# SwiGLU gating on one core: the first tile's store cut into 4 KiB and 28 KiB per partition

## The chip, the cores and the metric

One core of a Trainium2 chip. The time is device microseconds of one execution, the median over several. The profiled span is about 1.8 us shorter than the time of the same execution (933.9 against 935.7), so the two are not mixed below.

## The reference

```python
x: (8192, 8192) float32
a, b = np.split(x, 2, axis=-1)
return a * (b / (1 + np.exp(-b)))          # (8192, 4096) float32
```

268 MB are read and 134 MB written, with three operations per output element.

## The kernel before

Two rows of `x` are laid side by side in one partition, so a tile is 128 partitions of 64 KiB, and its result 32 KiB per partition, written over the front of the tile. Three tiles fit. SyncE issues the loads, ScalarE the stores of all but the last two tiles. Each of these two engines has its own queue of transfers, called a ring below: SyncE's (q1 in the profile) is the load ring, ScalarE's (q10) the store ring.

```python
R, BUFS = 2, 3
xv = x.tensor.reshape([N // R, R * M]).ap()
ov = out.tensor.reshape([N // R, R * half]).ap()

def swiglu(i, k, c0=0, cw=half):            # row k of tile i
    b = xt[:, k * M + half + c0 : ...]
    nc.scalar.activation(out=b, in_=b, func=_SILU)
    nc.vector.tensor_mul(out=xt[:, k * half + c0 : ...], in0=xt[:, k * M + c0 : ...], in1=b)

def store(i, c0=0, cw=R * half):
    (nc.scalar if i < last - 1 else nc.sync).dma_start(
        out=ov[i * P : (i + 1) * P, c0 : c0 + cw], in_=tiles[i][:, c0 : c0 + cw])

nc.vector.memset(zt, 0.0)                              # zt: 128 x 128
nc.scalar.dma_start(out=ov[0:P, 0:128], in_=zt)        # the early zero store, overwritten later

for i in range(BUFS):
    load(i)
for i in range(last):
    for k in range(R):
        swiglu(i, k)
    if i == last - 1:
        swiglu(last, 0)
    store(i)
    nxt = i + BUFS
    if nxt < last:
        load(nxt)
    ...                                                # the last tile is loaded by rows
... # cut: the last tile, in halves of a row, and its two stores
```

Of the kernel before, what the change touches and what calls it, by code (L numbers as in the profile page):

```python
# [1 line left out]

# [4 lines left out]

_SILU = mybir.ActivationFunctionType.Silu


@with_exitstack
def kernel(
    ctx: ExitStack,
    tc: tile.TileContext,
    x: bass.AP,
    out: bass.AP,
):




    nc = tc.nc
    N, M = x.shape
    half = M // 2
    P = nc.NUM_PARTITIONS
    R = 2
    BUFS = 3

    xv = x.tensor.reshape([N // R, R * M]).ap()  # L30
    ov = out.tensor.reshape([N // R, R * half]).ap()
    ntiles = N // (P * R)
    last = ntiles - 1

    pool = ctx.enter_context(tc.tile_pool(name="sbuf", bufs=BUFS))
    tiles = {}

    def load(i, rows=None):
        if i not in tiles:
            tiles[i] = pool.tile([P, R * M], x.dtype, name="xt")  # L40
        lo, hi = (0, R) if rows is None else rows
        nc.sync.dma_start(  # L42
            out=tiles[i][:, lo * M : hi * M], in_=xv[i * P : (i + 1) * P, lo * M : hi * M]
        )

    def swiglu(i, k, c0=0, cw=half):
        xt = tiles[i]
        b = xt[:, k * M + half + c0 : k * M + half + c0 + cw]
        nc.scalar.activation(out=b, in_=b, func=_SILU)  # L49
        nc.vector.tensor_mul(  # L50
            out=xt[:, k * half + c0 : k * half + c0 + cw],
            in0=xt[:, k * M + c0 : k * M + c0 + cw],
            in1=b,
        )

    def store(i, c0=0, cw=R * half):
        (nc.scalar if i < last - 1 else nc.sync).dma_start(
            out=ov[i * P : (i + 1) * P, c0 : c0 + cw], in_=tiles[i][:, c0 : c0 + cw]
        )


    zt = ctx.enter_context(tc.tile_pool(name="zeros", bufs=1)).tile([P, 128], x.dtype, name="zt")
    ctx.enter_context(tc.manual_schedule())
    nc.vector.memset(zt, 0.0)  # L64
    nc.scalar.dma_start(out=ov[0:P, 0:128], in_=zt)

    for i in range(BUFS):
        load(i)
    for i in range(last):
        for k in range(R):  # L70
            swiglu(i, k)
        if i == last - 1:
            swiglu(last, 0)
        store(i)
        nxt = i + BUFS
        if nxt < last:
            load(nxt)
        elif nxt == last:
            load(last, (0, 1))
            load(last, (1, 2))  # L80

    store(last, 0, half)
    for c0 in range(0, half, half // 2):
        swiglu(last, 1, c0, half // 2)
    store(last, half, half)


# [1 line left out]
_INS = ['x']  # L89
_OUTS = [((8192, 4096), 'float32')]  # L90


# [23 lines left out]
```

## Time and profile before

| | before |
|---|---|
| time, median of 3 | 935.86 us (935.71 to 936.21) |
| VectorE, ScalarE busy | 30%, 25% |
| packets of the two DMA queues | 68.6% + 31.2% of 16 engines' span |
| mean rate | 431 GB/s |

The DMA row and the two queue lines come first here, because they say that there is almost no idle time to win. The compute engines wait for data, and their idle time costs nothing. The prediction shows the lines and reads them. A "packet" below is one entry of the trace's DMA records, with its queue, start and duration. In this kernel it is one row of one partition, or the 4 bytes that report a transfer's end on one engine.

### The profile page before, as it was taken

The numbers are of one execution on the slowest core, as the hardware profiler recorded it, in microseconds if no ns is written. First come the engines' busy times: TensorE is split into PE (matmuls) and PEld (weight loads), VectorE is DVE, ScalarE is ACT, GpSimd is POOL, SyncE is SP. The second block draws the span as 40 slices with busy tenths as digits, with TensorE's granted clock in tenths as the row PEclk, the third lists the DMA queues.
The fourth block names the chain that finished last, engine by engine and source line by source line (L and its number), as shares of the span: only waits on it lengthen the run. The fifth ranks groups of instructions, "written<-read, shape, count | busy, mean of one in ns | idle before, by whom it ended". The sixth has DMA issues, their size and how long they took to land.

```text
span 933.9 us, 370 instructions
## 1 busy us (share of the span) xinstructions
DVE 283.5 (30%) x66; ACT 229.4 (25%) x66; POOL 0.2 (0%) x4
## 2 busy tenths in 40 slices
DVE  0333312333113332133321333213332133331252
ACT  0323330233312333113331133311333203332041
POOL 0000000000000000000000000000000000000000
DMA  9999999999999999999999999999999999999998
GB/s 407 422 413 460 411 431 441 449 427 420 456 408 445 431 431 441 435 422 441 448 414 436 435 451 425 429 443 414 446 427 436 436 432 425 439 451 411 441 434 383
DMA packets 9650, 402.74 MB, mean 431 GB/s; under 512 B 1072, under 2 KB 1200, under 8 KB 1200
## 3 DMA queue, kind: packets, MB, share of 16 engines
q1 hardware_dynamic: 5184, 276.83, 68.6%
q10 hardware_dynamic: 4464, 125.90, 31.2%
q14 instruction: 2, 0.02, 0.0%
HBM read 268.44 MB, written 134.28 MB: 431 GB/s over the span
## 4 chain that ended last, share of the span: by engine, by line
DMA 84%; DVE 10%; ACT 4%; DVEq 0%; issue 0%; SPq 0%; ACTq 0%
DMA out_dram<-xt 43%; DMA xt<-in_x_dram 41%; DVE xt L50 10%; ACT xt L49 4%; DVEq L111 0%; SPq L42 0%; ACTq L49 0%; DVEq L50 0%
## 5 line engine op out<-in xcount | busy, mean ns | idle before, releaser
L50 DVE TENSOR_TENSOR xt<-xt 128x4096 f32<-128x4096 f32 (+1 forms) x65 | 283.3, 4360 | 635.8 <-ACT xt L49 632.6
L49 ACT ACTIVATE xt<-xt 128x4096 f32<-128x4096 f32 (+1 forms) x65 | 228.1, 3556 | 686.5 <-DMA xt<-in_x_dram 686.5
L49 ACT ACT_TABLE_LOAD x1 | 1.3, 1283 | 1.5 <-DVE zt L64 1.5
L64 DVE MEMSET zt<- 128x128 f32 x1 | 0.2, 165 | 0.8 <-PEq L100 0.8
L100 POOL MEMSET const-bfloat16-1.0<- 128x1 bf16 x1 | 0.1, 101 | 0.0
L100 POOL MEMSET const-uint8-127<- 128x1 uint8 x1 | 0.1, 101 | 0.0
L100 POOL MEMSET const-float32-0.0<- 128x1 f32 x1 | 0.1, 98 | 0.2 <-issue 0.2
L100 POOL MEMSET const-float32-1.0<- 128x1 f32 x1 | 0.1, 98 | 0.0
## 6 DMA issues: line engine op xcount, KB each, us to landing
out_dram<-xt ACTq DMA_DIRECT2D x30, 4096.0 KB, 40.0
xt<-in_x_dram SPq DMA_DIRECT2D x2, 4096.0 KB, 26.8
out_dram<-xt SPq DMA_DIRECT2D x1, 4096.0 KB, 23.6
out_dram<-xt SPq DMA_DIRECT2D x2, 2048.0 KB, 14.5
xt<-in_x_dram SPq DMA_DIRECT2D x31, 34.2
out_dram<-zt ACTq DMA_DIRECT2D x1, 64.0 KB, 24.1
```

What stands on the lines that cost most here:

```text
L49: nc.scalar.activation(out=b, in_=b, func=_SILU)
L50: nc.vector.tensor_mul(out=xt[:, k * half + c0 : k * half + c0 + cw], in0=xt[:, k * M + c0 : k * M + c0 + cw], in1=b,)
L64: nc.vector.memset(zt, 0.0)
L100: nc = _bacc.Bacc("TRN2", target_bir_lowering=False, num_devices=1)
```

## The change

The intent: some output leaves as soon as the first row of the first tile is multiplied, rather than after both rows, so that the store ring starts earlier and with small packets.

```diff
-    def swiglu(i, k, c0=0, cw=half):
+    def swiglu(i, k, c0=0, cw=half, gated=None):
         nc.scalar.activation(out=b, in_=b, func=_SILU)
+        if gated:
+            gated()
         nc.vector.tensor_mul(...)
 ...
     for i in range(last):
-        for k in range(R):
-            swiglu(i, k)
+        swiglu(i, 0)
+        if i == 0:
+            swiglu(i, 1, gated=lambda: store(0, 0, half // 4))
+        else:
+            swiglu(i, 1)
         if i == last - 1:
             swiglu(last, 0)
-        store(i)
+        if i == 0:
+            store(i, half // 4, R * half - half // 4)
+        else:
+            store(i)
```

## The prediction

> **What bounds the kernel now.** I read the page's busy line first, then its DMA queues, then the stretches of time, then the chain and the first 75 us of the timeline.
>
> The page of before:
>
> ```profile
> DVE 283.5 (30%) x66; ACT 229.4 (25%) x66; POOL 0.2 (0%) x4
> ...
> DMA  9999999999999999999999999999999999999998
> ...
> q1 hardware_dynamic: 5184, 276.83, 68.6%
> q10 hardware_dynamic: 4464, 125.90, 31.2%
> ...
> HBM read 268.44 MB, written 134.28 MB: 431 GB/s over the span
> ...
> out_dram<-xt ACTq DMA_DIRECT2D x30, 4096.0 KB, 40.0
> ...
> xt<-in_x_dram SPq DMA_DIRECT2D x31, 34.2
> ```
>
> VectorE and ScalarE are idle for 70% or more. The 16 DMA engines are at 90% or more in 39 of 40 slices, and the packets of the two queues fill 68.6 + 31.2 = 99.8% of their span. q1 carries what SyncE issues (all loads, the last three stores), q10 what ScalarE issues (the other stores). A store takes 40.0 us from issue to landing and a load 34.2, though either alone would need 4.19 MB / 431 GB/s = 9.7 us or 19.5 us: most of it is queueing behind the other ring and behind the transfer ahead.
>
> Now the stretches, with busy times of the engines, then the DMA share and GB/s at the end of a line:
>
> ```profile
> 100.00:400.00 300.00, 91.01 (x21) 77.37 (x22) 0.00 (x0) 1.00 1.00 432
> 400.00:700.00 300.00, 94.85 (x22) 72.19 (x21) 0.00 (x0) 1.00 1.00 435
> ...
> 35.40:45.70 10.30, 0.00 (x0) 0.01 (x1) 0.00 (x0) 1.00 0.95 366
> ...
> 932.00:934.00 2.00, 0.00 (x0) 0.00 (x0) 0.00 (x0) 1.00 0.02 8
> ```
>
> From 100 us on the share is 1.00. What isn't full is the start, the stretch in which the first store joins (366 GB/s; a stretch this short also has some rounding of packets at its edges) and the 2.0 us after the last bytes. The timeline gives the start that the change touches:
>
> ```profile
> 22.77 7.12 ACT L49 ACTIVATE xt<-xt 128x4096 f32<-128x4096 f32 x2 [20.03 <-DMA xt<-in_x_dram]
> 26.42 8.95 DVE L50 TENSOR_TENSOR xt<-xt 128x4096 f32<-128x4096 f32 x2 [25.43 <-ACT xt L49]
> 35.40 0.34 ACTq L57 DMA_DIRECT2D out_dram<-xt  x1
> 45.69 7.12 ACT L49 ACTIVATE xt<-xt 128x4096 f32<-128x4096 f32 x2 [15.79 <-DMA xt<-in_x_dram]
> ```
>
> The packet records of the same trace are more exact. A load row of 64 KiB is one packet and takes 2.418 us on its engine, a store row of 32 KiB 1.213 us, a 512 B row of the zero store 0.027 us, and from about 40 us on each engine takes one packet of q1, one of q10, and so on. Each engine has 256 x 2.418 + 256 x 1.213 = 929.5 us of packets, and the last of them ends 929 to 930 us after the first began. So the span is the sum of the packets, plus some 1.2 us before the first, plus some 2 us of landing after the last, plus two small excesses: the first load packet is 0.4 to 0.9 us too long, and the load packet that is under way when the first 32 KiB store packets arrive (36 to 39 us) takes 3.0 to 3.6 us instead of 2.418, some 0.6 to 1.1 us once, with up to 1 us more one packet later on a few engines; about 1.0 us on each. I call that the entry bubble. It is all of the 933.9 us that the change can reach.
>
> The chain of waits says "DMA 84%; DVE 10%": store, load of the same buffer, SiLU, two multiplies, store. That loop takes 40.4 + 33.8 + 3.6 + 2 x 4.4 = 86.7 us for three tiles, 28.9 us a tile, and the packets of one tile take 8 x (2.418 + 1.213) = 29.05 us. It is one loop seen twice: the landings are long because the engines are full. Shortening the compute part of it would only lengthen the queueing.
>
> **What the Trainium skill says.** "DMA: Bandwidth & Descriptors", section "Issuing engines are not separate DMA queues", says that transfers run on the same 16 DMA engines and interleave, whichever engine issued them. The trace agrees: 431 GB/s with two queues, and either queue alone also runs at 2.418 us per 64 KiB. The same page, "Queues, rings and completion order", says that an engine takes the queues in turn at packet granularity; the trace agrees one packet for one packet, and this makes the packet size the store's share. The page's "Where 436 GB/s comes from" puts the ceiling at 435.2 GB/s; the stretch from 400 to 700 us shows 435. No page that I read has the entry bubble.
>
> **The change, part by part.**
>
> (a) Removed: nothing. Instructions: ScalarE's stream has one DMA issue more (0.34 us on ScalarE's sequencer, before a wait for VectorE that it has anyway). The second SiLU is issued ahead of the new store, so the store doesn't hold it up. The compiled order shows otherwise the same operations in the same order on every engine. The new first part takes over the wait for the zero store (landed at about 25 us, so it costs nothing); the second part waits for VectorE alone, not for the first part; the load into the first buffer waits for both parts.
>
> (b) Moved: the first 4 KiB of each row leave when the first multiply ends, 26.42 + 4.43 = 30.85 us, not at 35.40, so 4.5 us earlier, while two loads are queued and the engines are busy. No byte is added, and nothing idles there that the early bytes could fill.
>
> (c) Added packets: 8 per engine. From the two sizes, 2 x 1.213 - 2.418 = 0.008 us is the fixed part of one, and 4 KiB and 28 KiB take about 0.16 and 1.06 us. Eight extra plus one more completion: 8 x 0.008 + 0.01 = under 0.1 us.
>
> (d) Changed interleaving. Working through one engine by hand: eight 4 KiB packets, each behind a 2.418 us load packet, occupy the store ring from about 34 us to 52. The 28 KiB packets queue behind them in order and start about 54.5 us, where before the first store was half done. The second and third loads, less slowed, end about 41.7 (before 44.5) and 65.0 (before 73.5). The first store ends about 70.3, not 66.2, so the fourth load is issued about 72 us, not 69.8, and the load ring is empty from 65 to 73: four or five packets of the next store (issued about 55.5) run alone. The engine remains full throughout. After that both rings are fed again, loads with a lead of about 10 us (before 3.7), stores with about 3 (before 8). That is the same stock of three buffers, placed otherwise: store landings should fall from 40.0 to about 34 us and load landings rise from 34.2 to about 40.
>
> (e) End: the last two stores of SyncE stand behind the last load in the same ring, and 9.7 + 4.9 us of their packets cover the compute of the last half row, 6.5 us from landing to issue. That slack of several us isn't touched.
>
> Sum: +0.1 us of packets, +0 of idle engines, and the entry bubble, which I can't derive: 1.0 us is there now.
>
> **The rivals.**
>
> 1. The bubble shrinks. The 512 B packets of the zero store entered at about 7 us and left the load packets beside them at 2.418, so the bubble goes with the size of the entering packet. If 4 KiB enters nearly free and 28 KiB then finds a ring that is already running, 0.6 to 0.9 us are won: 935.1.
>
> 2. The bubble only moves to the first 28 KiB packet, being the filling of a second stream's buffering: +0.1 us, 935.95. For it: the bubble comes to about 1 us, near the time of one 32 KiB packet.
>
> 3. The bubble belongs to any ring that restarts beside a running one. Then the load ring's restart at about 73 us adds another, and a store ring that falls dry once or twice another: +0.5 to +1.8 us, 936.4 to 937.6. Against it: in the tail the other ring ends and the stream goes from loads to stores without a gap; but no restart after 40 us exists in before.
>
> 4. A large loss from the late first store (a load ring dry for 8 us). If nothing else filled the engines, +8 us, 944. Against it: the second store is in the queue since about 56 us, and it fills them. Even this would be within 2%.
>
> 5. A gain from earlier store bytes, 4.5 us off the chain and so 931. Against it: the engines have 929.5 us of packets, and the ends cost over 3.
>
> **Range and chances.** Weights 0.35 for rival 1, 0.35 for 2, 0.25 for 3 and little for the rest give a middle of 935.9. The three runs of before lie 0.5 us apart, which widens both sides a little: 935.0 to 937.1. Faster by 2% would mean 917 us, below the sum of the packets: 0.003. Slower by 2% would need 19 us of idle engines or slower packets: 0.007. Within 2%: 0.99.
>
> **What would show it.** The timeline of the changed kernel should have two ScalarE store issues at about 30.9 and 35.4 us, the second SiLU pair of tile 1 about 43 instead of 45.7, and the wait of the fourth load ending near 72. The DMA row should stay at nines, the steady stretch at 432 to 435 GB/s. Median landings should be swapped, about 34 for stores and 40 for loads. The packet records should show bubbles (or none) at 34 and 54 us (rivals 1 and 2) and at 73 us (rival 3). I'd be wrong if a stretch after 100 us has a share under 1.00, if the 64 KiB packets are longer than 2.418 us in the new phase, or if the last store is issued so late that the final stretch has a gap.

## The result

The changed kernel took 936.72 us (median of 6, 936.36 to 936.88), the kernel before 935.79 us in the same rounds (median of 6, 935.67 to 936.65). The ratio is 1.0008, with a 95% interval of 0.9995 to 1.0021: the same within 2%. A ratio here is the mean time of one kernel's fast runs over that of the other's fast runs of the same rounds, so it isn't quite the ratio of the medians.

The page of the changed kernel, the lines that answer to those of before:

```profile
DVE 283.4 (30%) x66; ACT 229.4 (25%) x66; POOL 0.2 (0%) x4
...
DMA  9999999999999999999999999999999999999998
...
q1 hardware_dynamic: 5184, 276.83, 68.5%
q10 hardware_dynamic: 4608, 125.90, 31.2%
...
HBM read 268.44 MB, written 134.28 MB: 431 GB/s over the span
...
out_dram<-xt ACTq DMA_DIRECT2D x29, 4096.0 KB, 34.4
...
out_dram<-xt ACTq DMA_DIRECT2D x1, 3584.0 KB, 37.6
out_dram<-xt ACTq DMA_DIRECT2D x1, 512.0 KB, 24.5
xt<-in_x_dram SPq DMA_DIRECT2D x31, 39.8
```

The bytes are the same, and q10 has 144 packets more: 128 rows and 16 completions. The engines are as full as before. The first part of 0.5 MB needed 24.5 us from issue to landing, and the median landings have changed places (stores 40.0 to 34.4, loads 34.2 to 39.8).

The timeline of the changed kernel (start and length in us, engine, line, operation):

```profile
26.52 8.95 DVE L52 TENSOR_TENSOR xt<-xt 128x4096 f32<-128x4096 f32 x2 [25.53 <-ACT xt L49]
30.98 4.87 ACTq L59 DMA_DIRECT2D out_dram<-xt  x2
42.71 7.12 ACT L49 ACTIVATE xt<-xt 128x4096 f32<-128x4096 f32 x2 [12.71 <-DMA xt<-in_x_dram]
...
68.92 7.12 ACT L49 ACTIVATE xt<-xt 128x4096 f32<-128x4096 f32 x2 [19.09 <-DMA xt<-in_x_dram]
...
73.22 51.02 SPq L42 DMA_DIRECT2D xt<-in_x_dram  x3
...
106.28 7.12 ACT L49 ACTIVATE xt<-xt 128x4096 f32<-128x4096 f32 x2 [30.24 <-DMA xt<-in_x_dram]
```

The two store issues begin at 30.98 us. The second tile is there at 42.71 instead of 45.69, and the third at 68.92 instead of 74.56, because the store ring's small packets take little from them. The price is the fourth load: its issue waits for the first store until 73.22 us, and its tile is there at 106.28 instead of 103.71. The lines of before:

```profile
69.83 29.28 SPq L42 DMA_DIRECT2D xt<-in_x_dram  x2
74.56 7.12 ACT L49 ACTIVATE xt<-xt 128x4096 f32<-128x4096 f32 x2 [21.75 <-DMA xt<-in_x_dram]
...
103.71 7.12 ACT L49 ACTIVATE xt<-xt 128x4096 f32<-128x4096 f32 x2 [22.03 <-DMA xt<-in_x_dram]
```

Steady state, from 100 us on:

```profile
100.00:400.00 300.00, 88.99 (x21) 75.36 (x22) 0.00 (x0) 1.00 1.00 435
400.00:700.00 300.00, 96.85 (x22) 74.20 (x21) 0.00 (x0) 1.00 1.00 435
```

The DMA share is 1.00, as before.

One engine, worked out from the packet records (start in us and duration in ns; L is a load, S a store, with KiB; us are counted here from 1.25 us before the first load packet, which is within half a microsecond of the profile's):

```
before   34.02 L64 2418 | 36.44 L64 3272 | 39.71 S32 1213 | 40.92 L64 2424 | 43.34 S32 1213 | ...
after    34.10 L64 2418 | 36.52 S4 159 | 36.67 L64 2418 | 39.09 S4 159 | 39.24 L64 2418 | ...
         52.25 L64 2418 | 54.67 L64 3211 | 57.88 S28 1062 | 58.94 L64 2418 | 61.35 S28 1062 | ...
         65.89 S28 | 66.95 S28 | 68.00 S28 | 69.06 S28 | 70.12 S28 | 71.19 S32 | 72.40 S32 |
         73.61 S32 | 74.82 S32 | 76.03 S32 | 77.23 L64 2418 | 79.65 S32 1213 | ...
```

The 4 KiB packets enter without stretching the load packets beside them. The stretched packet, the "entry bubble" of the prediction, is there all the same, 18 us later, in front of the first 28 KiB packet: 3.21 us instead of 2.42. From 66 to 77 us the load ring is dry, and ten store packets run back to back. The engine is never idle, and the load ring's return at 77.23 costs nothing.

So where do 0.9 us come from? The span can be cut into four pieces: to the first packet; from there to the mean end of the last packets of the 16 engines; from the mean to the slowest engine; and from there to the end of the program (here the start of its last instruction). Before: 1.74 + 930.33 + 0.61 + 1.21. After: 1.75 + 930.24 + 1.25 + 1.56. The body isn't longer. The slowest engine is 0.63 us later behind the mean, and the program takes 0.34 us more to end.

In these two traces the slowest engine can be followed back packet by packet, and it never waited more than 0.01 us between two. After, it had lost 2.02 us in the entry bubble (0.53 and 1.50 in two load packets), where the mean over the engines was 0.86. Before, it had lost 0.85 us there and 0.53 in one load packet at 437 us, beside a packet that fetched instructions.

The last piece is visible in the view of the source line that holds the end of the program: the SyncE instructions of it, before and then after (count; shortest, median and longest in ns; first and last start in us).

```profile
L111 SPq EVENT_SEMAPHORE  x6: 17/28/12459, 920.5 to 933.9; - x6
...
L111 SPq DRAIN  x3: 7/7/7, 933.2 to 933.5; - x3
```

```profile
L120 SPq EVENT_SEMAPHORE  x6: 17/28/12551, 921.0 to 934.8; - x6
...
L120 SPq DRAIN  x3: 7/7/129, 933.8 to 934.5; - x3
```

The long wait, for the last store, ends at 920.5 + 12.46 = 932.96 us before and at 921.0 + 12.55 = 933.55 after. From there to the end of the span it is 1.0 us before and 1.3 after. One of SyncE's three drains took 129 ns instead of 7, and the three lie 0.7 us apart instead of 0.3. By the exact records the stretch from the last landing to the end is 0.88 against 1.22 us.

### The profile page after: what moved, and what is told of

The parts are those of the page before. It is cut to its first block, busy times and chain, and to the rows that moved or that the text cites. A ratio compares the mean times of both kernels' runs of the same rounds, so it can differ in the third digit from the quotient of the medians.

```text
span 934.8 us, 375 instructions
## 1 busy us (share of the span) xinstructions
DVE 283.4 (30%) x66; ACT 229.4 (25%) x66; POOL 0.2 (0%) x4
## 4 chain that ended last, share of the span: by engine, by line
DMA 84%; DVE 10%; ACT 4%; DVEq 0%; issue 0%; SPq 0%; ACTq 0%
DMA xt<-in_x_dram 47%; DMA out_dram<-xt 37%; DVE xt L52 10%; ACT xt L49 4%; DVEq L120 0%; SPq L42 0%; ACTq L49 0%; DVEq L52 0%
## 6 DMA issues: line engine op xcount, KB each, us to landing
out_dram<-xt ACTq DMA_DIRECT2D x29, 4096.0 KB, 34.4
out_dram<-xt ACTq DMA_DIRECT2D x1, 512.0 KB, 24.5
xt<-in_x_dram SPq DMA_DIRECT2D x31, 39.8
```

## The experiments

Twelve runs followed, each for five timed rounds against the kernel before on the same chip (e1 to e8 on one chip, e9 to e12 on another). Three of them repeat a kernel on purpose, and one turned out to. The differences are so small that the traces carry the verdicts. I had two theories. Theory A, later narrowed to M: the packets and the bubble are what they were, and the difference is made at the end, by the program's end and the slowest engine. Theory B: the swapped leads of the two rings, or the load ring's dry stretch, cost something every time. A ring's lead is the work that is queued ahead on it, and the longer it is, the later a transfer lands after its issue; so the landings show it. Each trace was cut into the pieces above. "Entry" is the mean per engine of what load packets took over 2.418 us when the stores came in.

| kernel | median us | unchanged kernel, same rounds | entry bubble us, at us | mean end | slowest behind it | last landing to end |
|---|---|---|---|---|---|---|
| before | 935.86 | | 1.11, 33 to 42 | 930.33 | 0.61 | 0.88 |
| after | 936.72 | 935.79 | 0.86, 51 to 57 | 930.24 | 1.25 | 1.22 |
| e1 after again | 936.75 | 935.93 | 1.11, 51 to 57 | 930.46 | 0.72 | 1.22 |
| e2 (same program) | 936.89 | 935.93 | 1.06, 51 to 57 | 930.55 | 0.87 | 1.22 |
| e3 first row early | 936.83 | 935.93 | 1.10, 33 to 42 | 930.41 | 1.31 | 1.22 |
| e4 ramp | 936.40 | 935.93 | 0.70, 57 to 63 | 930.25 | 0.84 | 1.04 |
| e5 two zero stores | 936.64 | 936.28 | 1.13, 45 to 51 | 930.49 | 0.70 | 1.03 |
| e6 after, no zero store | 936.54 | 936.28 | 1.03, 51 to 57 | 930.37 | 1.62 | 0.95 |
| e7 before, no zero store | 935.85 | 936.28 | 1.17, 36 to 39 | 930.32 | 0.63 | 0.81 |
| e8 late first store | 936.39 | 936.28 | 0.89, 42 to 48 | 930.67 | 1.23 | 0.96 |
| e9 before, tiny load | 937.18 | 936.24 | 1.00, 33 to 39 | 930.72 | 0.71 | 1.22 |
| e10 before again | 936.54 | 936.24 | 1.10, 33 to 39 | 930.52 | 1.36 | 0.88 |
| e11 after, tiny load | 937.09 | 936.24 | 1.21, 51 to 57 | 930.64 | 1.43 | 1.24 |
| e12 after, third time | 937.20 | 936.24 | 0.85, 51 to 60 | 930.42 | 1.88 | 1.22 |

Mean end is the mean, over the 16 engines, of the end of each one's last data packet, in us from the first packet of the program. (The expectations of e1 and e10 quote 930.34, 930.36 and lags of 1.1 and 0.6: these were means over the 16 latest packets, some of which were on the same slow engine. The expectations of e5, e6 and e8 count the end from the last bytes, 0.33 us before the landing.) One trace stands behind each row, so a single value of the last three columns says little. What repeats does.

**e1, the changed kernel again.**

> The changed kernel again, on this chip. The first runs gave 936.7 against 935.8, more than their own spread but 0.1%, and the packets added account for under 0.1 us. Theory A (the tail: the mean end of the 16 engines is the same in both traces, 930.34 and 930.36 us after the first packet, but the slowest engine is last by 1.1 us instead of 0.6, because its entry bubble was larger; then the completion): the sign may change from run to run and the median difference shrinks to 0.3 or less. Theory B (the swapped leads of the two rings, or the load ring running dry once, cost something every time): again +0.7 to +1.0 us. The entry bubble of about 0.8 us should again lie at 54 us, at the first 28 KiB packets, and the load ring's restart at 77 us should again show none.

936.75 against 935.93: 0.82 us again, so the difference is not chance, and A's "0.3 or less" was wrong. The bubble was again at 51 to 57 us, and there was none at the load ring's return. The end took 1.22 us again. The slowest engine was only 0.72 us behind the mean this time.

**e2, the split without the early issue (a miss).**

```diff
-            swiglu(i, 1, gated=lambda: store(0, 0, half // 4))
+            swiglu(i, 1)
+            store(0, 0, half // 4)
```

> The split without the early issue: both parts are issued after the second multiply, at about 35.4 and 35.7 us. It tells the split from the early issue. If the early issue costs (an extra interleaving of small packets from 31 us on): back to 935.8. If the split costs through the swapped leads (theory B): the first store ends later than in the changed kernel, near 75 us, the load ring is dry longer, and the time is at or above 936.7, up to 937.5. Theory A: 935.8 to 936.8 with no relation to it. In all of them the small packets should enter at about 39 us without a bubble, and the first 28 KiB packets near 59 us with one of 0.8 us.

The compiled instructions of all engines, with their waits, turned out to be those of the changed kernel: ScalarE's stream has the second SiLU, then the store, either way, and the store waits only for the first multiply. The timeline has the issues at 30.90 us. So the `gated` hook of the change does nothing to the instructions, and this run is a repeat: 936.89 us, end 1.22. It says nothing of the early issue.

**e3, the whole first row early.**

```diff
-  store(0, 0, half // 4)  ...  store(i, half // 4, R * half - half // 4)
+  store(0, 0, half)       ...  store(i, half, R * half - half)
```

> The first part is the whole first row, 16 KiB per partition, issued at 31 us; the rest is 16 KiB. If the bubble grows with the entering packet and comes once: a bubble of 0.3 to 0.5 us at about 36 us, none at the second 16 KiB part. If it is the filling of a store stream's buffer up to the packet's size: 0.3 to 0.5 at 36 us and the rest, 0.4 to 0.5, when the first 32 KiB packets come (about 70 us). If it is a fixed price for the first packet over some size: 0.8 to 1.0 at 36 us. The first store should land before 66 us, the load ring shouldn't fall dry, and theory B then expects 935.8; theory A expects 935.5 to 936.5.

The bubble came at the 16 KiB packets and came whole: 1.10 us over the first few load packets between 33 and 42 us, and nothing when the 32 KiB packets followed near 71 us. So it is neither proportional to the packet nor paid again for growth. It is a price paid once, and 4 KiB packets don't trigger it. I had expected the load ring not to fall dry, which was wrong: sixteen packets per engine took the store to 71 us, as in the changed kernel. Landings were 34.4 and 39.8, and the time 936.83.

**e4, a ramp of 4, 8 and 20 KiB.**

```diff
-            store(i, half // 4, R * half - half // 4)
+            store(i, half // 4, half // 2)
+            store(i, 3 * half // 4, R * half - 3 * half // 4)
```

> The rest of 28 KiB is cut again: 8 KiB, then 20 KiB, so the packets of the store ring grow 512 B, 4, 8, 20, 32 KiB. If a bubble is paid for the growth of the packet over what has been seen (filling), the parts sum to the same 0.8 to 1.0 us: about 0.1 at 8 KiB, 0.3 to 0.4 at 20 KiB, 0.3 to 0.4 at 32 KiB. If only the first large one pays, one bubble of 0.4 to 0.6 at 20 KiB and nothing after it. The load ring is dry for longer (the first store takes 24 packets per engine, so it ends near 90 us): theory B expects 937 to 938, theory A 935.8 to 936.8 as the engines stay full of the next store.

The bubble came with the 8 KiB packets: 0.70 us at 57 to 63 us. Before that the 4 KiB packets cost 0.14 us together, and afterwards two load packets at 75 us cost 0.07 us. The sum, about 0.9, is within the range of the others (0.85 to 1.21). The first store didn't end near 90 us, as I had written, but at 71: the 20 KiB packets met a dry load ring and ran alone. The time was uneven, 935.99 to 937.92. Two transfers more, four waits at the end, and still only 1.04 us from landing to end: no drain was slow here.

```profile
L121 SPq DRAIN  x3: 7/7/7, 933.5 to 933.8; - x3
```

**e5, one transfer more in the kernel before (a miss).**

```diff
-    nc.scalar.dma_start(out=ov[0:P, 0:128], in_=zt)
+    nc.scalar.dma_start(out=ov[0:P, 0:64], in_=zt[:, 0:64])
+    nc.scalar.dma_start(out=ov[0:P, 64:128], in_=zt[:, 64:128])
```

> The kernel before, with its zero store cut into two of 256 B rows, so that it has one transfer more, as the changed kernel has, but its first store whole and at 35 us. In the traces so far the changed kernel and its relatives need 1.55 us from the last bytes on the slowest engine to the end of the program, the kernel before 1.21: one more wait for a semaphore of SyncE and a drain of SyncE of about 0.13 us that comes 0.2 us later. Theory M (the program's end, shifted by the number of transfers or of instructions): these 0.3 us return here, and the time is about 936.2. Theory B (swapped leads or the late first store): leads and landings as before (stores 40, loads 34), so 935.9.

The timeline and the landings of this run:

```profile
45.00 0.34 ACTq L57 DMA_DIRECT2D out_dram<-xt  x1
45.38 7.12 ACT L49 ACTIVATE xt<-xt 128x4096 f32<-128x4096 f32 x2 [15.21 <-DMA out_dram<-zt]
...
58.02 0.34 ACTq L57 DMA_DIRECT2D out_dram<-xt  x1
```

```profile
out_dram<-xt ACTq DMA_DIRECT2D x30, 4096.0 KB, 33.9
...
xt<-in_x_dram SPq DMA_DIRECT2D x31, 40.1
out_dram<-zt ACTq DMA_DIRECT2D x2, 32.0 KB, 33.9
```

The first store was issued at 45.00 instead of 35.40 us: it waits for what wrote the same output before, and the second zero store, eight more packets per engine each behind a load packet, needed over 40 us. The bracket of the second line names it. So the leads swapped here too, and the run can't separate the theories. It shows something else: swapped leads need no split. The time was 936.64 against 936.28, the end 1.03.

**e6, the changed kernel without the zero store.**

```diff
-    nc.scalar.dma_start(out=ov[0:P, 0:128], in_=zt)
```

> The changed kernel without the zero store: the number of transfers is that of the kernel before. Theory M: the end takes 1.2 us again and the time is 936.2 to 936.4, of which the rest over 935.9 would be the slowest engine. Theory B: 936.7 as before. The entry: if the 512 B packets of the zero store had prepared the store ring, the 4 KiB packets now show a bubble of up to 0.8 us at 34 to 36 us; if the bubble goes by packet size alone, still none there and 0.8 to 1.0 us at 54 us.

The end took 0.95 us, near that of the kernel before, no drain was slow, and the difference fell to 0.26 us (936.54 against 936.28), though the leads stayed swapped (34.3 and 39.9). That speaks for M and against B, though e10 below shows that two medians of one program can lie 0.30 us apart. The 4 KiB packets again entered with about 0.1 us, and the bubble of 1.03 us came at 51 to 57: the zero store prepares nothing.

**e7, the kernel before without the zero store.** The same edit to the kernel before.

> The kernel before without the zero store. If the zero store prepares nothing, the same bubble of about 1.0 us at 36 to 40 us and the time within 0.3 us of 935.9 (its 8 small packets are 0.2 us per engine). If it shortens the entry of the first real store, a bubble of 1.3 to 2 us and a time of 936.2 to 937.

Bubble 1.17 us, end 0.81, time 935.85 against 936.28. The early zero store buys nothing that these runs show. This kernel has the lowest median of the twelve runs, but the ratio (0.9998, interval 0.9985 to 1.0012) doesn't set it apart from the kernel before, so there is no version here that beats both for certain.

**e8, the first store whole but late.**

```diff
+    def late():
+        store(0)
+        load(BUFS)
     for i in range(last):
         for k in range(R):
-            swiglu(i, k)
+            swiglu(i, k, gated=late if (i, k) == (1, 0) else None)
+        if i == 0:
+            continue
```

> The kernel before with its first store whole but issued late, after the first SiLU of the second tile, about 49 us instead of 35. By the count of packets the first store then ends near 71 us, the load ring is dry from about 65 to 76 us and the leads of the two rings are swapped (stores about 34, loads about 40 us to landing), all as in the changed kernel, without split, extra transfer or small packets. Theory B: 936.7. Theory M: 935.9, end of 1.2 us. In both one entry bubble of 0.8 to 1.1 us near 51 to 55 us. If the larger lag of the slowest engine belongs to an entry at that time, about 936.4.

The landings and the end of the program in this run:

```profile
out_dram<-xt ACTq DMA_DIRECT2D x30, 4096.0 KB, 34.2
...
xt<-in_x_dram SPq DMA_DIRECT2D x31, 40.0
```

```profile
L119 SPq DRAIN  x3: 7/7/7, 934.2 to 934.5; - x3
```

The issue was at 42.17 us, not 49: the second tile came sooner than I had worked out, and the store left when that tile's SiLU began (42.11), not when it ended. The leads are those of the changed kernel, without a split or a transfer more, and the median is 936.39 against 936.28: 0.11 us, not B's 0.8 to 0.9. It is the clearest run against B. It does show one thing that the changed kernel lacked: when the load ring came back at 75 us, 15 engines lost 0.31 us (mean over 16), a small form of the prediction's third rival.

**e9 to e12, two by two.** A tiny load that nobody reads, 64 B per partition, was put behind the third load, in the kernel before (e9) and in the changed one (e11). e10 and e12 are the two kernels unchanged, beside them.

```diff
     for i in range(BUFS):
         load(i)
+    nc.sync.dma_start(out=tl, in_=xv[0:P, 0:16])
```

> The kernel before with one transfer more that touches nothing else: 64 B per partition, loaded on SyncE's ring behind the third load and read by nobody. The two zero stores of the fifth run turned out to hold the first store back to 44 us, so that run told nothing of the transfer count alone; this one keeps the first store at 35 us and the leads as they were (stores 40, loads 34). Theory M (transfer count shifts the end): from the last landing to the end 1.0 to 1.22 us against 0.88, time over that of the unchanged kernel by 0.15 to 0.35 us. Theory B: no difference.

> The kernel before under a label of its own, for a second trace: last landing to end 0.88 us again if that belongs to the kernel and not to chance; the slowest engine 0.6 us behind the mean of the 16 if the tight end is a property of the old phase, 0.6 to 1.4 as in the kernels with swapped leads if it is chance. The entry bubble again about 1.1 us at 36 to 40 us, as a mean of the engines.

> The changed kernel with the same tiny load: two transfers more than before. The ramp, which also had two more, waited for four semaphores after the last landing but had no slow drain, and took 1.04 us instead of 1.22. Theory M: 1.0 to 1.1 us here too, and a time 0.1 to 0.2 us under that of the changed kernel, in spite of one transfer more. If the count alone mattered, 1.28.

> The changed kernel a third time, beside the other three: 1.22 us from the last landing to the end, bubble 0.8 to 1.1 us at 51 to 57 us. The difference to the unchanged kernel of these rounds: 0.34 us if only the end protocol differs for good; 0.8 to 0.9 again if the slowest engine or the phase adds 0.5 us every time. The slowest engine then should be 0.6 to 1.2 us behind the mean.

The SyncE drains at the end, e9 and e10:

```profile
L113 SPq DRAIN  x3: 7/7/116, 933.8 to 934.4; - x3
```

```profile
L111 SPq DRAIN  x3: 7/7/7, 934.2 to 934.5; - x3
```

In e9 the kernel before has the slow drain and an end of 1.22 us, from a tiny load alone, and its time is 937.18: the whole difference of the changed kernel, with its first store whole and at 35 us. It isn't as clean as I meant it to be: the tiny packets held the load ring while eight store packets passed, the leads swapped (34.2 and 40.0), and 0.41 us were lost near 87 to 91 us. In e10 the kernel before has its end of 0.88 us again, but a slowest engine 1.36 us behind the mean, where the first trace had 0.61: that piece varies within one kernel. Its median, 936.54, is 0.30 us over that of the same program in the same rounds, so a difference of that size is noise. Its leads in this run were 38.0 and 36.3, so they too can drift in one kernel. In e11 I expected the end to shrink to about 1.05; it took 1.24, with a drain of 116 ns. So the number of transfers alone isn't the rule: two more gave 1.04 in the ramp and 1.24 here. e12: 937.20 against 936.24 and 936.54, with an end of 1.22.

**What the twelve runs say together.** Seven traces have a drain of 116 to 130 ns in their end and 1.22 to 1.24 us from landing to end: the changed program in its four traces (after, e1, e2, e12), e3, e9 and e11. Their medians are 0.82 to 0.96 us over the unchanged kernel of the same rounds. Six runs have no slow drain (e4 to e8 and e10), an end of 0.81 to 1.04, and medians from 0.43 under to 0.47 over. The end itself accounts for 0.34 us of the changed kernel's difference, and it repeated in every trace of the same program (1.22 in four of four, 0.88 in two of two).

The records hold a link that has no exception in the fourteen traces. SyncE's stream has 81 instructions in the seven with the slow drain, 79 in before, e7 and e10, and 80 in e4, e5, e6 and e8. From the start of SyncE's last instruction before its third drain to the start of its very last one, it is 0.46 us with 79, 0.54 to 0.55 with 80 and 0.73 with 81. So 0.27 of the 0.34 us goes with two instructions more on SyncE, and the other 0.07 with one more semaphore that it waits for. That is a link and not a cause: no run gave SyncE an instruction more without another transfer or wait.

What stays open: why the drain is slow at 81, and the other 0.5 to 0.6 us. The obvious place is the slowest engine, and in the first pair of traces it is there (0.63 us). But it doesn't hold over repeats: over four traces of the changed program the last packet ended 931.18 to 932.30 us after the first, over two of the unchanged one 930.95 and 931.88. The means, 931.6 and 931.4, differ by 0.2 us, less than either spread.

## Why the prediction was right or wrong

The time, 936.72 us, lies in the range of 935.0 to 937.1, and "within 2%" held. The point, 935.9, was 0.8 us low. That the range held the time is in part luck: its part above 936.4 was there for rival 3, which didn't happen, and the longer end of the program that helped to put the time there is in none of the rivals.

- What bounds the kernel: right. The same packets fill the same engines before and after, and moving a store 4.5 us earlier (30.98 instead of 35.40) moved no idle time, because there is none.
- (b) and (d), the moves: right, most of them to a microsecond or so. Second tile 42.7 (worked out "about 43"), fourth load's issue 73.2 ("about 72"), first store's last packet at 71.2 ("about 70.3"), load ring dry from 66 to 77 ("65 to 73"), landings 34.4 and 39.8 ("about 34" and "about 40"). The lengths of rows alone, 2.418, 1.213 and 0.16 us, and turn by turn alternation gave nearly all of that. The end of the dry stretch is the exception, 4 us later than worked out: the fourth load's first packets started 3.9 to 4.5 us after its issue.
- (c), the packets: right. 159 + 1062 - 1213 = 8 ns for each of eight, and a completion.
- The entry bubble: rival 2. It moved to the first 28 KiB packets and remained about 1 us (0.85 to 1.11 in four traces of the changed program, 1.10 and 1.11 in two of the unchanged one). Rival 1 is refuted: a small entering packet doesn't save it. Rival 3 is refuted for this change, though e8 and e9 had 0.31 and 0.41 us at a restart. The reason given for rival 2, that the bubble's size is that of a packet being buffered, is not supported: 8 KiB packets and 16 KiB packets pay about the same 0.7 to 1.1 us. What the bubble is stays open. Neither the 944 of rival 4 nor the 931 of rival 5 came.
- (e), the last stores: held. The slowest engine ran from its bubble to its last packet without a gap over 0.01 us.
- The term that was mis-sized is the end. The sum has "+0.1 us of packets, +0 of idle engines" and the bubble, and nothing for the program's end, which "some 2 us of landing after the last" took as fixed. The end is set by the slowest of 16 engines and by the program's closing instructions, and the closing part grew by 0.34 us. The rest of the 0.8 us isn't settled. Also off, though it canceled: 1.74 us before the first packet in the kernel before, not "some 1.2", and 1.21 after the last, not "some 2".

## What to carry to other kernels

When the two DMA queues' packets add up to 99.8% of the span, an earlier transfer of the same bytes can't gain more than the few stretched packets at the edges, here about 1 us of 934. Count packets and durations on one engine: that predicts landings and swapped leads well, but for differences of about a tenth of a percent also look at the slowest engine and at the instructions after the last landing, and take several traces before believing either. Check the compiled order before calling something an experiment: one of mine compiled to the kernel it was meant to differ from, and two others moved the very thing that they were meant to hold still.

## What the Trainium skill lacked or had wrong

- "DMA: Bandwidth & Descriptors", "Queues, rings and completion order": it gives a packet as about 9 to 17 descriptors, typically. Here an engine changes rings after a single row, one of 64 KiB (2.418 us) and one of 32 KiB (1.213 us) in turn, so the size of a row decides how the two rings share the engine. How many descriptors a row is, these records don't show.
- The same page has no entry bubble: a store ring that brings its first packets of 8 KiB or more beside a running load ring stretches the load packets by 0.7 to 1.2 us per engine in all, once. 512 B packets showed none, and 4 KiB packets at most about 0.14 us.
- No page that I read says that the stretch from the last landing to the end differs between programs that move the same bytes: 0.81 to 1.24 us here, with a SyncE drain of 7 ns in some and 116 to 130 ns in others.
- "Runtime: NRT & Kernel Launch", "Instruction fetch mechanics", has instructions fetched in 16 KiB blocks at a cost that is mostly hidden, and says nothing of the data packets beside them. In these traces two instruction packets of 8 KiB come at about 430 to 460 us, and beside them one load packet takes about 0.53 us and another about 0.25 us more, each on one engine alone. It isn't hidden when the engine that loses it is the slowest at the end, as the one that lost 0.53 us in the trace of before was.
